# Attention on pairs of key tiles in two adjacent PSUM banks: two double buffers in place of four single ones

## The chip, the cores and the metric

The kernel runs on one core of a Trainium2 chip. The metric is the device time of one execution in microseconds. In a profile, PE is TensorE's matmuls and PEld its weight loads, DVE is VectorE, ACT is ScalarE, POOL is GpSimd, SP is SyncE, which here only issues DMAs. L595 is line 595 of the kernel before.

## The reference

One encoder layer is applied to two requests of 2048 and 256 tokens, which the kernel treats as 2304 tokens in 18 tiles of 128:

```python
p = rmsnorm(x) @ w_in                       # mq mk mv mo gates aq ak av
m_out = mlstm_mixer(mq, mk, mv, mo, gates)  # 8 heads of 64, both directions
a_out = attention_mixer(aq, ak, av)         # 8 query heads, 2 key/value heads of 64
x = x + concat([m_out, a_out]) @ w_out
u = dwconv3(rmsnorm(x) @ w_up);  a, g = split(u)
x = x + (silu(g) * a) @ w_down
```

The attention is a full softmax over the keys of the own request, without a mask:

```python
s = einsum('bqhgd,bkhd->bhgqk', q, k) * HEAD_DIM ** -0.5
o = einsum('bhgqk,bkhd->bqhgd', softmax(s, axis=-1), v)
```

## The kernel before, in words

The program has four phases. Phase A makes queries, keys, values and gates and writes them to DRAM. Then attention runs beside the mLSTM; when the mLSTM has nothing more to issue, phase C (the output projection, its matmuls `po` at L1041) takes its place beside the rest of the attention. Phase D is the feed-forward part.

**Attention.** It is a generator, `attention`, that works through 36 blocks. A block holds four query tiles of 128 (512 query columns) that share a key/value head. 32 blocks are large: their keys are the 16 tiles of the long request. Four are small: two key tiles. Counted from 0, blocks 0, 1, 26 and 27 are small. A large block has eight steps `kp`, each for a pair of key tiles. In a step

- `scores` computes for each key tile z of the pair one score tile `ps` of 128 keys x 512 queries in one PSUM bank, by two matmuls (L595, L596; the second adds the low part and the subtraction of the row maximum). ACT writes the exp in rounded form to `ph` (L599), then the full exp in place (L600), and DVE takes the difference `pl` (L601).
- `maxstep` belongs to the next block: a matmul of queries against 512 keys into `px` (L569) and a maximum over its columns on DVE (L570). A large block needs 16 of them, which are spread over the first steps (the count `k`).
- `values` multiplies `ph` and `pl` of an earlier step by the values, six matmuls into `pv` (L613).

Around a block stand the transposes of the queries into `pq` (L555), the transposed maxima `pr` (L584), and at its end four reciprocals of 64x128 (L630) and a multiplication on POOL. The tiles `ps`, `px`, `pq` and `pr` share one tag of the PSUM pool, with `SCB = 4` buffers of one bank. `ph` and `pl` have six buffers each, that is three steps.

**What sets the order.** `run_both` advances the two generators by the costs that they yield, so that the mLSTM is issued ahead of the attention by a factor `LEAD`. The program is built by a scheduler with a timeline of its own: it takes instructions from the issued order and places one on an engine once its inputs and its buffer are free in that timeline; otherwise a later one goes first. So the order on PE is fixed when the program is built, and PE then runs it strictly in turn. After the mLSTM's last step is issued, PE's order is the one in which the code is written (`manual_schedule`); from there `po` matmuls are dealt out between the attention's steps. The mLSTM's matmuls are `mj`, `mv` (projections, 128x256 each, the bulk), `mS`, `mI`, `mN`, `mu`, `mt`, `mT` (the recurrence).

Of the kernel before, what the change touches and what calls it, by code (L numbers as in the profile page):

```python
# [9 lines left out]
F32 = mybir.dt.float32  # L10
F32R = mybir.dt.float32r
AF = mybir.ActivationFunctionType
ALU = mybir.AluOpType
AX = mybir.AxisListType
# [3 lines left out]
P = 128  # L18
# [11 lines left out]
ACOL = 2048  # L30
MPRI = 2000
STORE = "sync"
SCB = 4
MB = 2
MJ = 1
BLK = 768
# [25 lines left out]
A_MAX = 0.23  # L62
# [9 lines left out]
RW = 4  # L72
PO = 4
PB = 4
PHB = 6
PLB = 6
PLAG = 2
ZT = 3
SG = 3
# [9 lines left out]
def f32(ap):  # L89
    return ap.bitcast(F32)  # L90
# [382 lines left out]
def attention(g, tc, s1, s2, pp):  # L473


    nc = g.nc
    sp = s1
# [13 lines left out]
    def load_kv(grp, k0, k1, after=None):  # L491

        if (grp, k0) in kv:
            return
        n = k1 - k0
        sp = s2 if n == NT1 else s1
        kv[(grp, k0)] = parts = []
        for t0 in range(0, n, 4):
            m = min(4, n - t0)
            s = f"{n}_{t0}"  # L500
            kk = sp.tile([P, m * P], F32R, tag="kk" + s, name=f"kk{grp}_{s}", bufs=1)
            kl1 = sp.tile([65, m * P], F32R, tag="kl1" + s, name=f"kl1{grp}_{s}", bufs=1)
            vs = [sp.tile([P, m, P if a == 0 else HD], F32R, tag=f"v{a}" + s, name=f"v{a}{grp}_{s}", bufs=1)
                  for a in range(2)]
            c = slice((k0 + t0) * P, (k0 + t0 + m) * P)
            if after is not None:
                for t in (kk[0:1, 0:1], kk[HD:HD + 1, 0:1], kl1[0:1, 0:1], vs[0][0:1, 0, 0:1], vs[1][0:1, 0, 0:1]):
                    nc.gpsimd.tensor_copy(t, after[0:1, 0:1])
            nc.gpsimd.memset(f32(vs[0][:, :, HD:]), 1.0)
            for r in (0, HD):  # L510
                nc.gpsimd.dma_start(f32(kk[r:r + HD, :]), g.k_d[grp, 0:HD, c])
            nc.gpsimd.dma_start(f32(kl1[0:HD, :]), g.k_d[grp, HD:P, c])
            nc.gpsimd.memset(f32(kl1[64:65, :]), 1.0)
            for a in range(2):
                nc.gpsimd.dma_start(f32(vs[a][:, :, 0:HD]), g.v_d[a, grp, :, k0 + t0:k0 + t0 + m])
            parts.append((kk, kl1, vs))
# [14 lines left out]
    def load_q(n):  # L531

        if n in qzs or n >= len(hbs):
            return
        t = 0
        qz = qzs[n] = sp.tile([P, 4, P], F32R, tag="qz", name=f"bq{n}", bufs=QZB)
        for h, q0, q1 in hbs[n][1]:
            nc.sync.dma_start(f32(qz[:, t:t + q1 - q0]), g.q_d[q0:q1, :, h].rearrange("n p d -> p n d"))
            t += q1 - q0

    def prep(n):

        s = HB()
        grp, s.qs, k0, k1 = hbs[n]
        load_q(n)
        load_q(n + 1)
        load_kv(grp, k0, k1)
        s.kv = kv[(grp, k0)]
        s.nq, s.nk = 4, k1 - k0
        s.N = s.nq * P  # L550
        s.nm = "%d_%d" % s.qs[0][0:2]
        qz = qzs.pop(n)
        pq = pp.tile([P, 512], F32R, tag="sc", name="pq" + s.nm)
        for t in range(s.nq):
            nc.tensor.transpose(pq[:, t * P:(t + 1) * P], qz[:, t, :], g.identr)  # L555
        s.qq = sp.tile([P, 512], F32R, tag="qq", name="qq" + s.nm, bufs=2)
        nc.scalar.activation(s.qq[:, 0:s.N], f32(pq[:, 0:s.N]), AF.Copy)
        s.qm = sp.tile([65, 512], F32R, tag="qm", name="qm" + s.nm, bufs=2)
        nc.scalar.activation(s.qm[0:HD, 0:s.N], f32(pq[0:HD, 0:s.N]), AF.Copy)
        s.mx = sp.tile([P, 4, 4], F32, tag="mx", name="mx" + s.nm, bufs=2)  # L560
        s.nsp = -(-s.nk * P // 512)
        s.todo = [(t, z) for z in range(s.nsp) for t in range(s.nq)]
        return s

    def maxstep(s):
        t, z0 = s.todo.pop(0)
        w = min(512, s.nk * P - z0 * 512)
        ps = pp.tile([P, 512], F32, tag="sc", name=f"px{s.nm}_{t}_{z0}")
        nc.tensor.matmul(ps[:, 0:w], s.qq[:, t * P:(t + 1) * P], s.kv[z0][0][:, 0:w], start=True, stop=True)  # L569
        nc.vector.tensor_reduce(s.mx[:, t, z0:z0 + 1], ps[:, 0:w], AX.X, ALU.max)  # L570

    def prep2a(s):

        nq = s.nq
        s.m4 = sp.tile([P, 4], F32, tag="m4", name="m4" + s.nm, bufs=2)
        nc.vector.tensor_reduce(s.m4[:, 0:nq], s.mx[:, 0:nq, 0:s.nsp], AX.X, ALU.max)
        s.m4r = sp.tile([P, 4], F32R, tag="m4r", name="m4r" + s.nm, bufs=2)
        nc.vector.tensor_scalar(s.m4r[:, 0:nq], s.m4[:, 0:nq], -1.0, None, ALU.mult)

    def prep2b(s):  # L580

        pr = pp.tile([P, 512], F32, tag="sc", name="pr" + s.nm)
        for t in range(s.nq):
            nc.tensor.matmul(pr[:, t * P:(t + 1) * P], s.m4r[:, t:t + 1].to_broadcast([P, P]), g.identr, start=True,  # L584
                             stop=True)
        nc.scalar.activation(s.qm[HD:HD + 1, 0:s.N], pr[HD:HD + 1, 0:s.N], AF.Copy)

    def scores(s, kp):
        N = s.N
        parts = []  # L590
        for z in range(2):
            ps = pp.tile([P, 512], F32, tag="sc", name=f"ps{s.nm}_{kp}_{z}")[:, 0:N]
            kk, kl1, _ = s.kv[kp // 2]
            kc = (2 * kp + z) % 4 * P
            nc.tensor.matmul(ps, kk[:, kc:kc + P], s.qq[:, 0:N], start=True, stop=False)  # L595
            nc.tensor.matmul(ps, kl1[:, kc:kc + P], s.qm[:, 0:N], start=False, stop=True)  # L596
            ph, pl = (sp.tile([P, 512], F32R, tag=t, name=f"{t}{s.nm}_{kp}_{z}", bufs=n)[:, 0:N]
                      for t, n in (("ph", PHB), ("pl", PLB)))
            nc.scalar.activation(ph, ps, AF.Exp)  # L599
            nc.scalar.activation(ps, ps, AF.Exp)  # L600
            nc.vector.tensor_tensor(pl, ps, f32(ph), ALU.subtract)  # L601
            parts.append((ph, pl))
        return parts

    def values(s, kp, parts):

# [41 lines left out]

    g.a_total = sum(A_PAIR * pairs(b) + A_MAX * 4 * -(-pairs(b) // 2) + A_PREP for b in hbs)
    cur = prep(0)  # L650
    while cur.todo:
        maxstep(cur)
        yield A_MAX
    prep2a(cur)
    prep2b(cur)
    load_kv(0, 0, NT1, cur.m4)
    todo, fins = [], []

    def value():

        s, kp, parts = todo.pop(0)
        values(s, kp, parts)
        if kp == s.nk // 2 - 1:
            while fins:
                fins.pop(0)()
            fin1(s)
            fins.extend([lambda: fin2(s)] * 4 + [lambda: fin3(s), lambda: fin4(s)])

    for n in range(len(hbs)):
        nxt = prep(n + 1) if n + 1 < len(hbs) else None  # L670
        yield A_PREP / 2
        nkp = cur.nk // 2
        ready = None
        for kp in range(nkp):
            todo.append((cur, kp, scores(cur, kp)))
            yield 0.4 * A_PAIR
            if ready:
                prep2b(ready)
                ready = None
            if nxt is not None and nxt.todo:  # L680
                if n == len(hbs) // 2 - 1:

                    k = 2 * (kp - 2) - (nxt.nq * nxt.nsp - len(nxt.todo))
                else:
                    k = -(-len(nxt.todo) // max(nkp - kp - (MXZ if g.alone else MXE), 1))
                for i in range(k):
                    maxstep(nxt)
                    if i % 2:
                        yield 2 * A_MAX
                if not nxt.todo:  # L690
                    prep2a(nxt)
                    ready = nxt
            if len(todo) > PLAG:
                value()
                yield 0.6 * A_PAIR
            for _ in range(1 if kp < nkp - 1 else 2):
                if fins:
                    fins.pop(0)()
        if nxt is not None and nxt.todo:
            while nxt.todo:  # L700
                maxstep(nxt)
# [690 lines left out]
def body(tc, aps, phases="abcd"):  # L1392
# [5 lines left out]
    with ExitStack() as st:  # L1398
# [3 lines left out]
        def pool(stack, name, **kw):  # L1402
            return stack.enter_context(tc.tile_pool(name=name, reuse_waits="tile", **kw))
# [25 lines left out]
        with ExitStack() as s2:  # L1429
# [34 lines left out]
            sa = pool(s2, "b_s", bufs=2)  # L1464
            pa = pool(s2, "b_p", bufs=SCB, space=PSUM)

# [117 lines left out]
```

## Time and profile before

| | |
|---|---|
| three runs, us | 3429.24, 3425.78, 3429.64; median 3429.24 |
| span of the profiled execution, us | 3427.2 (its own time is not listed; the runs' median is 2.0 above the span) |
| busy share PE, DVE, ACT, POOL | 97%, 78%, 56%, 33% |
| instructions | 55596 |
| score matmuls, two per key tile (L595, L596) | 1040 |
| exps (L599, L600), 128x512 | 1040 |
| differences (L601), 128x512 | 520 |
| row maxima (L570) | 528 |

Time runs along the span: phase A until about 250 us, attention beside the mLSTM until about 1400, attention beside phase C until about 1770, then the rest. The row "granted clock" tells at what share of its full speed PE's clock was let through. In the groups, "busy" is the sum over a group, then the mean of one; "idle before" is the time in which the engine stood still just ahead of these instructions, with what ended it.

### The profile page before, as it was taken

What the parts mean: (1) busy time and instruction counts of PE and PEld (TensorE: products, weight loads), DVE (VectorE), ACT (ScalarE), POOL (GpSimd) and SP (SyncE); (2) the same over time, 40 slices, a digit from 0 to 9 for tenths busy, and PEclk for the clock granted to TensorE, in tenths of its full rate; (3) what the DMA queues carried; (4) which work ended last, traced back from release to release, by engine and by line L of the source; (5) the groups of instructions that cost most, each with busy time, mean ns of one, the idle gap of its engine ahead of it and who ended that gap; (6) DMA issues with size and microseconds to landing.
All of it is one profiled execution on the core that took longest, in us unless ns stands there. A gap on an engine that the chain in (4) does not pass through costs nothing. (4 is left out here: it accounts for less than half of the span.)

```text
span 3427.2 us, 55596 instructions
## 1 busy us (share of the span) xinstructions
PE 3329.3 (97%) x20058; PEld 3098.4 (90%) x20058; DVE 2677.3 (78%) x4654; ACT 1931.2 (56%) x4329; POOL 1120.9 (33%) x1328
## 2 busy tenths in 40 slices
PE   7989999999999999899999999999999999999998
PEld 6878888888888888688899999999999999999998
DVE  6885687777768788967767878789888888888776
ACT  4536666666666767655544444446444446555554
POOL 6653132213232323211244333226233224322222
PEclk9999999999999999999999999999999999999999
DMA  6765342333345444422365232223323213421221
GB/s 220 243 203 159 89 140 86 115 123 98 108 131 160 143 123 139 145 77 94 101 216 198 81 105 87 68 80 133 129 94 103 72 59 128 140 74 62 69 74 50
DMA packets 254756, 404.27 MB, mean 118 GB/s; under 512 B 32112, under 2 KB 156816, under 8 KB 254480
## 3 DMA queue, kind: packets, MB, share of 16 engines
q1 hardware_dynamic: 226576, 358.23, 32.7%
q0 software_dynamic: 11344, 33.04, 3.6%
q10 hardware_dynamic: 16560, 9.44, 0.9%
q8 instruction: 158, 2.59, 0.3%
q14 instruction: 118, 0.97, 0.1%
HBM read 316.73 MB, written 83.90 MB: 117 GB/s over the span
## 5 line engine op out<-in xcount | busy, mean ns | idle before, releaser
L1322 PE MATMUL pd<-act,wd 128*128 128x384 f32 (+1 forms) x3120 | 593.4, 336 | 23.9 <-DVE acc L1324 12.6
L1322 PEld LDWEIGHTS pd<-act,wd 128*128 128x128 f32 x3120 | 539.6, 188 | 32.6 <-DVE acc L1324 18.1
L601 DVE TENSOR_TENSOR pl<-ps,ph 128x512 fp32r<-128x512 f32 x520 | 352.7, 683 | 181.5 <-ACT ps L600 173.4
L1184 PE MATMUL pa<-nt,wut 128*128 128x386 f32 (+2 forms) x2376 | 454.3, 339 | 0.0
L599 ACT ACTIVATE ph<-ps 128x512 fp32r<-128x512 f32 x520 | 309.4, 595 | 243.5 <-PE ps L596 239.5
L1184 PEld LDWEIGHTS pa<-nt,wut 128*128 128x128 f32 x2376 | 421.6, 190 | 0.3 <-ACT u L1200 0.3
L570 DVE TENSOR_REDUCE mx<-px 128x1 f32<-128x512 f32 (+1 forms) x528 | 345.5, 670 | 74.4 <-PE px L569 72.4
L1278 DVE SCALAR_TENSOR_TENSOR y<-u,cw,y 128x768 f32<-128x768 f32 (+1 forms) x264 | 315.6, 1196 | 36.4 <-ACT y L1271 29.3
L1189 POOL TENSOR_TENSOR tw<-ru 128x512 f32<-128x512 f32 x66 | 94.1, 1425 | 732.5 <-DMA ru<-w_up 558.5
L613 PE MATMUL pv<-ph,v 128*128 128x512 f32 (+1 forms) x1040 | 319.4, 401 | 1.0 <-ACT ph L599 0.8
L600 ACT ACTIVATE ps<-ps 128x512 f32<-128x512 f32 x520 | 310.3, 597 | 0.0
L1200 ACT ACTIVATE u<-pa 128x386 f32<-128x386 f32 (+2 forms) x264 | 128.3, 486 | 320.9 <-PE pa L1184 320.7
L1324 DVE TENSOR_TENSOR acc<-pd,acc 128x384 f32<-128x384 f32 (+1 forms) x544 | 280.3, 535 | 35.5 <-PE pd L1322 34.1
L1041 PEld LDWEIGHTS po<-cmx,wo 128*128 128x128 f32 x1728 | 220.7, 191 | 8.2 <-DVE mmx L931 0.6
L1041 PE MATMUL po<-cmx,wo 128*128 128x256 f32 x1728 | 224.2, 284 | 0.4 <-DVE mmx L931 0.4
L595 PE MATMUL ps<-qq,kk 128*128 128x512 f32 x520 | 215.5, 416 | 4.2 <-DVE mx L570 2.4
L569 PE MATMUL px<-kk,qq 128*128 128x512 f32 (+1 forms) x528 | 202.8, 413 | 6.0 <-DVE mx L570 2.9
L596 PE MATMUL ps<-qm,kl 65*128 65x512 f32 x520 | 206.7, 399 | 0.0
L759 PE MATMUL mj<-mn,wm 128*128 128x256 f32 x1296 | 203.0, 289 | 2.8 <-ACT og L773 1.9
L759 PEld LDWEIGHTS mj<-mn,wm 128*128 128x128 f32 x1296 | 187.1, 193 | 19.8 <-ACT og L773 2.0
L769 PEld LDWEIGHTS mv<-wm,mn 128*128 128x128 f32 x1296 | 182.8, 190 | 18.4 <-ACT qb L765 2.5
L769 PE MATMUL mv<-wm,mn 128*128 128x256 f32 x1296 | 196.5, 285 | 1.0 <-ACT qb L765 0.9
(288 smaller groups left out, 7266.6 us busy)
## 6 DMA issues: line engine op xcount, KB each, us to landing
ru<-w_up SPq DMA_DIRECT2D x132, 512.0 KB, 3.4
mn<-n_d SPq DMA_DIRECT2D x216, 256.0 KB, 3.4
rd<-w_down SPq DMA_DIRECT2D x66, 512.0 KB, 3.6
n_d<-n1T SPq DMA_DIRECT2D x18, 1024.0 KB, 5.6
dm<-nm_d POOLq DMA_DIRECT2D x72, 256.0 KB, 4.1
mjn<-n_d SPq DMA_DIRECT2D x72, 256.0 KB, 3.3
mvn<-n_d SPq DMA_DIRECT2D x72, 256.0 KB, 3.1
q_d<-qz SPq DMA_DIRECT2D x18, 512.0 KB, 3.7
```

The costliest lines, as they stand in the source:

```text
L570: nc.vector.tensor_reduce(s.mx[:, t, z0:z0 + 1], ps[:, 0:w], AX.X, ALU.max)
L599: nc.scalar.activation(ph, ps, AF.Exp)
L600: nc.scalar.activation(ps, ps, AF.Exp)
L601: nc.vector.tensor_tensor(pl, ps, f32(ph), ALU.subtract)
L613: nc.tensor.matmul(s.pv[0:HD if k in (1, 3) else P, 0:N], v, p, start=(kp == 0 and k == 0), stop=(2 * kp + 2 == s.nk and k == 5))
L759: nc.tensor.matmul(pj[:, o], s.w[c][:, a, o * P:(o + 1) * P], nT[c][:, :, h, :], start=(c + o + k == 0), stop=(c == NCC - 1 and k == 2 and ...
L769: nc.tensor.matmul(pv[:, o], nT[c][:, o, a, :], s.w[c][:, h, 256:512], start=(c + o + k == 0), stop=(c == NCC - 1 and k == 2 and o == 1))
L1041: nc.tensor.matmul(po[:, o], wo[z // 2][c][:, a, n], mx[c][:, h, :], start=(c == 0 and k == 0), stop=(c == NCC - 1 and k == 2))
L1184: nc.tensor.matmul(p, w[:, aa, c, :], ops[k][:, c, bb, 0:n], start=c == 0 and i == 0 and not add, stop=c == NCC // 2 - 1 and i == 2, skip_ ...
L1278: nc.vector.scalar_tensor_tensor(y[:, s:e], u[:, s + k:e + k], cw[:, k, jj:jj + 1], y[:, s:e], ALU.mult, ALU.add)
L1322: nc.tensor.matmul(po, wds[j][c // 4][:, aa, c % 4 * P:(c % 4 + 1) * P], acts[j][:, bb, z0:z1], start=(j == 0 and k == 0), stop=(j == len( ...
L1324: nc.vector.tensor_tensor(accs[c][:, z0:z1], po, accs[c][:, z0:z1], ALU.add)
```

## The change

The two score tiles of a step become one tile of 128x2x512 in two adjacent banks. The four matmuls come first, then one exp to `ph`, one in place and one difference, each on 1024 columns. A `maxstep` takes two query tiles at once: two matmuls into the two banks, one maximum with two results. The shared tag has two buffers of two banks in place of four of one; `pq` and `pr` take a whole double buffer each. `ph` and `pl` have three double buffers. The matmuls stay as they are, in number and shape. `k` and the yields are scaled to the halved number of steps, so that as much cost is yielded as before.

```diff
-SCB = 4
+SCB = 2
-PHB = 6
-PLB = 6
+PHB = 3
+PLB = 3
...
-        pq = pp.tile([P, 512], F32R, tag="sc", name="pq" + s.nm)
+        pq = pp.tile([P, 2, 512], F32R, tag="sc", name="pq" + s.nm)[:, 0]
...
-        s.todo = [(t, z) for z in range(s.nsp) for t in range(s.nq)]
+        s.todo = [(t, z) for z in range(s.nsp) for t in range(0, s.nq, 2)]
...
-        ps = pp.tile([P, 512], F32, tag="sc", name=f"px{s.nm}_{t}_{z0}")
-        nc.tensor.matmul(ps[:, 0:w], s.qq[:, t * P:(t + 1) * P], s.kv[z0][0][:, 0:w], start=True, stop=True)
-        nc.vector.tensor_reduce(s.mx[:, t, z0:z0 + 1], ps[:, 0:w], AX.X, ALU.max)
+        ps = pp.tile([P, 2, 512], F32, tag="sc", name=f"px{s.nm}_{t}_{z0}")
+        for i in range(2):
+            nc.tensor.matmul(ps[:, i, 0:w], s.qq[:, (t + i) * P:(t + i + 1) * P], s.kv[z0][0][:, 0:w], start=True, stop=True)
+        nc.vector.tensor_reduce(s.mx[:, t:t + 2, z0], ps[:, :, 0:w], AX.X, ALU.max)
...
-        parts = []
+        ps = pp.tile([P, 2, 512], F32, tag="sc", name=f"ps{s.nm}_{kp}")[:, :, 0:N]
+        kk, kl1, _ = s.kv[kp // 2]
         for z in range(2):
...
+            nc.tensor.matmul(ps[:, z], kk[:, kc:kc + P], s.qq[:, 0:N], start=True, stop=False)
+            nc.tensor.matmul(ps[:, z], kl1[:, kc:kc + P], s.qm[:, 0:N], start=False, stop=True)
+        ph, pl = (sp.tile([P, 2, 512], F32R, tag=t, name=f"{t}{s.nm}_{kp}", bufs=n)[:, :, 0:N]
+                  for t, n in (("ph", PHB), ("pl", PLB)))
+        nc.scalar.activation(ph, ps, AF.Exp)
+        nc.scalar.activation(ps, ps, AF.Exp)
+        nc.vector.tensor_tensor(pl, ps, f32(ph), ALU.subtract)
+        return [(ph[:, z], pl[:, z]) for z in range(2)]
...
-                    k = 2 * (kp - 2) - (nxt.nq * nxt.nsp - len(nxt.todo))
+                    k = kp - 2 - (nxt.nq // 2 * nxt.nsp - len(nxt.todo))
...
                 for i in range(k):
                     maxstep(nxt)
-                    if i % 2:
-                        yield 2 * A_MAX
+                    yield 2 * A_MAX
```

With the buffers the scheduler's order changes over the whole stage. In the rows below a name holds the query tile at which the block begins, the step, before the change the key tile of the pair, and a running number; `x6` are six instructions of one kind. A wait names the engine whose semaphore is waited for.

PE beside the mLSTM, in the middle of the first key/value head (a block of query tile 4, step 3). Before:

```order
L595 MATMUL ps_4_3_1_5345<-qq_4_4510,kk_16_4_2662 128x512 [waits DVE_49]
L596 MATMUL ps_4_3_1_5345<-qm_4_4512,kl_16_4_2663 128x512
L769 MATMUL mv_1_6038<-wm_2_5222,mn_1_2_5969 128x256 x2
L769 MATMUL mv_1_6038<-wm_3_5223,mn_1_3_5970 128x256 x2
L569 MATMUL px_4_0_3_5365<-kk_16_12_2694,qq_4_5063 128x512 [waits DVE_49]
L769 MATMUL mv_1_6038<-wm_3_5223,mn_1_3_5970 128x256 x4
L769 MATMUL mv_1_6038<-wm_4_5224,mn_1_4_5971 128x256
L838 MATMUL mu_0_6521<-va_0_5280,kw_0_6242 128x130 [waits DVE_49,PE_49,Pool_49]
L769 MATMUL mv_1_6038<-wm_4_5224,mn_1_4_5971 128x256
L569 MATMUL px_4_1_3_5368<-kk_16_12_2694,qq_4_5063 128x512 [waits DVE_49]
```

The same block and step in the changed program:

```order
L596 MATMUL ps_4_3_5015<-qq_4_4282,kk_16_4_2658 128x512 [waits DVE_49]
L597 MATMUL ps_4_3_5015<-qm_4_4284,kl_16_4_2659 128x512
L596 MATMUL ps_4_3_5015<-qq_4_4282,kk_16_4_2658 128x512
L597 MATMUL ps_4_3_5015<-qm_4_4284,kl_16_4_2659 128x512
L613 MATMUL pv_4_5007<-pl_4_2_4866,v_16_4_2660 128x512 x2
L768 MATMUL mv_3_6407<-wm_5_4907,mn_3_5_6341 128x256 x6
L768 MATMUL mv_3_6407<-wm_6_4908,mn_3_6_6342 128x256
L900 MATMUL mN_10_6941<-va_5_2493,dm_10_6204 128x65 [waits DMASW4_49,Activation_49]
L882 MATMUL mS_11_6960<-qb_5_2492,mkT_5_2491 128x256 [waits PE_49,Activation_49]
L900 MATMUL mN_10_6941<-va_5_2493,dm_10_6204 128x65 x3
L571 MATMUL px_4_0_3_5037<-kk_16_12_2690,qq_4_4771 128x512 [waits DVE_49]
L571 MATMUL px_4_0_3_5037<-kk_16_12_2690,qq_4_4771 128x512
```

The attention's matmuls stand in groups, the mLSTM's stand in longer runs between them, and at the same step of the attention the mLSTM is two token blocks further on (`mv_3` in place of `mv_1`).

PE in block 22 of the 36 (second key/value head, query tile 4), from the end of step 0. Before:

```order
L613 MATMUL pv_2_14038<-pl_2_7_1_14337,v_16_12_11389 128x512 [waits DVE_49]
L569 MATMUL px_4_0_0_14432<-kk_16_0_11354,qq_4_14411 128x512 [waits Activation_49]
L838 MATMUL mu_8_15856<-va_4_13637,kw_8_15661 128x130 [waits DVE_49,Pool_49]
L569 MATMUL px_4_1_0_14435<-kk_16_0_11354,qq_4_14411 128x512 [waits Activation_49]
L569 MATMUL px_4_2_0_14438<-kk_16_0_11354,qq_4_14411 128x512 [waits DVE_49]
L838 MATMUL mu_9_15863<-va_4_13637,kw_9_15663 128x130 [waits Activation_49,Pool_49]
L569 MATMUL px_4_3_0_14441<-kk_16_0_11354,qq_4_14411 128x512 [waits DVE_49]
```

The same place in the changed program:

```order
L613 MATMUL pv_2_12756<-pl_2_7_13021,v_16_12_10393 128x512 x2
L571 MATMUL px_4_2_0_13114<-kk_16_0_10358,qq_4_13095 128x512 [waits DVE_49]
L571 MATMUL px_4_2_0_13114<-kk_16_0_10358,qq_4_13095 128x512
L613 MATMUL pv_4_13305<-ph_4_0_13105,v_16_0_10360 128x512 [waits PE_49,Activation_49]
L613 MATMUL pv_4_13305<-ph_4_0_13105,v_16_0_10361 64x512
L613 MATMUL pv_4_13305<-ph_4_0_13105,v_16_0_10360 128x512
L613 MATMUL pv_4_13305<-ph_4_0_13105,v_16_0_10361 64x512
L596 MATMUL ps_4_1_13258<-qq_4_12523,kk_16_0_10358 128x512 [waits DVE_49]
L597 MATMUL ps_4_1_13258<-qm_4_12525,kl_16_0_10359 128x512
L596 MATMUL ps_4_1_13258<-qq_4_12523,kk_16_0_10358 128x512
L597 MATMUL ps_4_1_13258<-qm_4_12525,kl_16_0_10359 128x512
L613 MATMUL pv_4_13305<-pl_4_0_13106,v_16_0_10360 128x512 x2
```

No mLSTM matmul is left here: in the changed order the last one (`mT_17` of the last head pair) stands in block 21, before the change in block 28. From block 22 to the first `po`, which in both programs stands in block 28, PE has attention alone.

DVE at the same place, from the first row maximum of step 0. Before:

```order
L570 TENSOR_REDUCE mx_4_14415<-px_4_2_0_14438 128x1 [waits PE_49]
L570 TENSOR_REDUCE mx_4_14415<-px_4_3_0_14441 128x1 [waits PE_49]
L630 RECIPROCAL rs_2_14619<-rs_2_14619 64x128 [waits Activation_49]
L630 RECIPROCAL rs_2_14619<-rs_2_14619 64x128 x3
L849 SCALAR_TENSOR_TENSOR C_9_13614<-C_8_13613,dec,C_9_13614 128x65 [waits Activation_49]
L601 TENSOR_TENSOR pl_4_1_0_14588<-ps_4_1_0_14584,ph_4_1_0_14587 128x512 [waits Activation_49]
```

In the changed program:

```order
L602 TENSOR_TENSOR pl_4_0_13106<-ps_4_0_13100,ph_4_0_13105 128x1024 [waits Activation_49]
L572 TENSOR_REDUCE mx_4_13099<-px_4_2_0_13114 128x2 [waits PE_49]
L630 RECIPROCAL rs_2_13283<-rs_2_13283 64x128 [waits Activation_49]
L630 RECIPROCAL rs_2_13283<-rs_2_13283 64x128 x3
L572 TENSOR_REDUCE mx_4_13099<-px_4_0_1_13268 128x2 [waits PE_49]
L602 TENSOR_TENSOR pl_4_1_13264<-ps_4_1_13258,ph_4_1_13263 128x1024 [waits Activation_49]
```

The four reciprocals stand in one piece in both; in the changed program they and a maximum stand ahead of the difference that frees the score buffer of step 1.

More of the change, by code (lines that the diff above doesn't have):

```diff
@@ L580, in prep2b @@
     def prep2b(s):
-        pr = pp.tile([P, 512], F32, tag="sc", name="pr" + s.nm)
+        pr = pp.tile([P, 2, 512], F32, tag="sc", name="pr" + s.nm)[:, 0]
         for t in range(s.nq):
@@ L589, in scores @@
         N = s.N
-        parts = []
+        ps = pp.tile([P, 2, 512], F32, tag="sc", name=f"ps{s.nm}_{kp}")[:, :, 0:N]
+        kk, kl1, _ = s.kv[kp // 2]
         for z in range(2):
-            ps = pp.tile([P, 512], F32, tag="sc", name=f"ps{s.nm}_{kp}_{z}")[:, 0:N]
-            kk, kl1, _ = s.kv[kp // 2]
             kc = (2 * kp + z) % 4 * P
[L595 to L603, printed above, removed]
+            nc.tensor.matmul(ps[:, z], kk[:, kc:kc + P], s.qq[:, 0:N], start=True, stop=False)
[6 more added lines that the diff above has]
+        return [(ph[:, z], pl[:, z]) for z in range(2)]
     def values(s, kp, parts):
@@ L652, in attention @@
         maxstep(cur)
-        yield A_MAX
+        yield 2 * A_MAX
     prep2a(cur)
@@ L687, in attention @@
                     maxstep(nxt)
-                    if i % 2:
-                        yield 2 * A_MAX
+                    yield 2 * A_MAX
                 if not nxt.todo:
```

## The prediction

> **What bounds the kernel now.** I read the head of the page first, then the busy times by stage, then what PE waits for in each stage.
>
> ```profile
> span 3427.2 us, 55596 instructions
> ...
> PE 3329.3 (97%) x20058; PEld 3098.4 (90%) x20058; DVE 2677.3 (78%) x4654; ACT 1931.2 (56%) x4329; POOL 1120.9 (33%) x1328
> ```
>
> The busy times of three stretches (busy and count for PE, PEld, DVE, ACT, POOL, then granted clock and DMA share):
>
> ```profile
> 400.00:1390.00 990.00, 986.13 (x6255) 863.84 (x6254) 771.41 (x1718) 674.78 (x1821) 284.34 (x577) 1.00 0.42 125
> 1390.00:1460.00 70.00, 59.43 (x292) 45.43 (x290) 63.61 (x151) 44.75 (x112) 10.47 (x20) 0.88 0.44 129
> 1460.00:1770.00 310.00, 305.41 (x1928) 268.22 (x1927) 215.66 (x371) 163.29 (x324) 63.90 (x67) 0.99 0.32 103
> ```
>
> PE stands still for only 3.9 us of the 990 in which attention has mLSTM work beside it. So there the time is PE's work, and DVE (78% busy) and ACT (68%) can become shorter without any gain. The one weak place is 1390 to 1460: the mLSTM runs out, PE is busy for 59.4 of 70 us, at a clock of 0.88, and DVE is the full engine with 63.6. PE's waits there, from the longest:
>
> ```profile
> PE mN L901 <- DVE mmx L931: 3.1, 1, 3.1
> PE px L569 <- DVE mx L570: 2.0, 4, 0.8
> ```
>
> This is what attention costs when nothing fills its waits. The 10.6 us of idle time and about 6 us by the lower clock (0.12 of 70 us is 8.4, part of it idle anyway) make some 16 us that PE loses there.
>
> **The removed cost.** The groups of the instructions that are merged:
>
> ```profile
> L601 DVE TENSOR_TENSOR pl<-ps,ph 128x512 fp32r<-128x512 f32 x520 | 352.7, 683 | 181.5 <-ACT ps L600 173.4
> ...
> L599 ACT ACTIVATE ph<-ps 128x512 fp32r<-128x512 f32 x520 | 309.4, 595 | 243.5 <-PE ps L596 239.5
> ...
> L570 DVE TENSOR_REDUCE mx<-px 128x1 f32<-128x512 f32 (+1 forms) x528 | 345.5, 670 | 74.4 <-PE px L569 72.4
> ```
>
> No operation on 1024 PSUM columns exists here, so I price it from other widths, by shape:
>
> ```profile
> L570 DVE TENSOR_REDUCE mx<-px 128x1 f32<-128x256 f32 x16 | 6.4, 418 | 2.1 <-PE px L569 1.6
> L254 ACT ACTIVATE qk<-pj 128x640 f32<-128x640 f32 x18 | 12.6, 701 | 19.3 <-DVE xh L273 9.9 <-PE pj L245 5.1 <-DMA mn<-n_d 3.1
> L186 ACT ACTIVATE xq<-x 128x1024 f32<-128x1024 f32 x16 | 16.8, 1060 | 28.5 <-DMA x<-xT 28.4
> L200 DVE TENSOR_TENSOR x<-x,rs_a 128x1024 f32<-128x1024 f32 x16 | 19.3, 1210 | 9.9 <-PE rs_a L142 9.9
> L630 DVE RECIPROCAL rs<-rs 64x128 f32<-64x128 f32 x144 | 122.4, 901 | 7.7 <-ACT rs L622 7.4
> L108 ACT ACTIVATE wo<-ro 128x512 fp32r<-128x512 f32 x16 | 9.9, 629 | 9.6 <-DMA ro<-w_out 9.0 <-PE mv L785 0.4
> L110 DVE TENSOR_TENSOR wo<-ro,wo 128x512 fp32r<-128x512 f32 x16 | 10.8, 686 | 1.9 <-ACT wo L108 1.8
> ```
>
> ACT: (701 - 595) over 128 columns is 0.83 ns a column, so 1024 columns take 1.02 us; the 640-column row crosses a bank, the 1024-column row (SBUF) gives 1.06 as upper bound. I take 1.02. DVE: the 512-wide maxima are 678 once the 16 narrow ones are taken out, so 260 ns for 256 columns and 1.2 us for 1024; the SBUF row says 1.21. Saved on paper: 260 x (2 x 683 - 1200) = 43 us and 264 x (2 x 678 - 1200) = 41 us of DVE, 520 x (2 x 595 - 1020) = 88 us of ACT. All of it is beside PE, which is busy in 986 of 990 us. I count it as zero; should that cover fail, the matter is the bare stage below. The mLSTM's loads on SP and POOL come earlier, with the same count; at a DMA share of 0.42 that costs nothing.
>
> **The added cost: a longer chain for a buffer.** How a step runs now, on PE, ACT and DVE:
>
> ```profile
> 1475.29 0.39 PE L595 MATMUL ps<-qq,kk 128*128 128x512 f32 x1
> 1475.52 0.40 PE L596 MATMUL ps<-qm,kl 65*128 65x512 f32 x1
> 1475.76 0.40 PE L595 MATMUL ps<-qq,kk 128*128 128x512 f32 x1
> 1476.00 0.40 PE L596 MATMUL ps<-qm,kl 65*128 65x512 f32 x1
> ```
>
> ```profile
> 1476.02 0.60 ACT L599 ACTIVATE ph<-ps 128x512 fp32r<-128x512 f32 x1 [3.02 <-PE ps L596]
> 1476.51 0.60 ACT L600 ACTIVATE ps<-ps 128x512 f32<-128x512 f32 x1
> 1477.03 0.59 ACT L599 ACTIVATE ph<-ps 128x512 fp32r<-128x512 f32 x1
> ```
>
> ```profile
> 1425.33 0.62 DVE L570 TENSOR_REDUCE mx<-px 128x1 f32<-128x512 f32 x1
> ...
> 1426.00 0.50 PE L595 MATMUL ps<-qq,kk 128*128 128x512 f32 x1 [1.29 <-DVE mx L570]
> ```
>
> Matmuls of 512 columns start every 0.235 us; ACT starts 0.10 after a score tile's end (1475.92) and the second exp 0.1 before the first one's end; PE starts 0.05 after DVE. A score tile of two banks thus needs: last matmul's end 3 x 0.235 + 0.40 = 1.10, then 0.10, exps 0.92 + 1.02, to 3.14; difference 0.04 + 1.20, to 4.38; next use at 4.43 us after its start. A `px` tile needs 0.24 + 0.40 + 0.04 + 1.2 + 0.05 = 1.9 us. Before, a single-bank score tile needed 0.64 + 0.1 + 0.5 + 0.6 + 0.04 + 0.68 + 0.05 = 2.6, with four buffers.
>
> *The stage with mLSTM work.* In the quoted rows of query tile 4 the score buffer is used again 39 matmuls after the tile's last one. At this stage's mean of 990/6255 = 0.158 us that is 6.2 us of work against 4.43 - 0.94 = 3.5 needed. So no wait is added where the runs are like this one: 0 us, with a bound of 60 us (below).
>
> *The bare stage.* The price of that order is that the mLSTM is used up by block 21. A large block of attention alone is 96 matmuls x 0.235 plus about 1 us for `pq` and `pr`, 23.5 us of PE work. Steps 0 to 3: score tiles come one chain apart, 4.43 us, for 14 matmuls (3.3 us); two `px` and the difference on DVE, 3.6 us, fit in. In step 1 four reciprocals (3.6 us) stand ahead of the difference; about 1 us of it falls in DVE's free time: +2.6. Together 20.3. Steps 4 to 7: two buffers, 2.2 us a step by the chain, 2.35 by PE (10 matmuls); I take 2.4, together 9.6. Change of block about 1. Sum 31.0, so 7.5 lost in each block:
>
> - blocks 22, 23, 24: 3 x 7.5 = 22;
> - block 21: 7.5, and eight weight splits of phase C on ACT (8 x 0.63) and DVE (8 x 0.69) put between its exps: +5, so 12;
> - blocks 25 to 28 until `po` begins: block 25 has no `px` of 512 columns but the reciprocals, 5; the small block 26 waits for its maxima and `pr`, 3; block 27 makes eight double `px` for block 28, 8 x 1.2 on DVE against 3.8 on PE, 7; five steps of block 28, 5: together 20;
> - the lower clock about block 27 (6, as now) and about 1 us in each bare block: 10.
>
> That is 64 us. The 16 us now lost at this place are replaced by it: +48. The least that the bare stage can cost is where chains overlap until DVE (16 x 1.2 + 3.6 = 22.8) or PE (23.5) is full: 1 us a block, some 25 in all with the small blocks and the clock, +9 net. The most is half clock throughout, below.
>
> *Blocks 17 to 20.* Some of the score buffers there are used again after only 2 to 3 us of matmuls: 59 score tiles, a quarter short by about 1.1 us, part of which coincides: +10 (0 to 20).
>
> *Beside phase C.* In 1460 to 1770 PE lost 4.6 us. Step 0 of a block has two `px` in a row on one buffer, a wait of some 1.2 us in each of seven blocks, 8: +4. In the other steps a buffer is used again after more than 4 us, no cost.
>
> Sum: 48 + 10 + 4 = +62. The profiled span is 3427.2, 2.0 below the median of the three runs (3425.78 to 3429.64); on the median the forecast is **3491 us**.
>
> [...] How the clock went in the bare part of today's kernel, in 10 us stretches:
>
> ```profile
> 1400.00:1410.00 10.00, 6.69 (x28) 5.79 (x27) 9.54 (x29) 4.55 (x12) 2.62 (x5) 0.50 0.40 108
> 1410.00:1420.00 10.00, 8.84 (x45) 6.23 (x44) 9.25 (x26) 7.45 (x25) 2.62 (x6) 1.00 0.08 24
> 1420.00:1430.00 10.00, 7.80 (x29) 5.13 (x28) 9.95 (x24) 5.81 (x14) 3.36 (x5) 0.86 0.09 25
> ```
>
> At 67% busy the clock was half, at 78% 0.86, at 88% full. The bare blocks would be 23.5/31 = 76% busy, 74% in steps 0 to 3. [...] The rows above agree that idling brings half clock in pieces; none shows it for a whole block. [...]
>
> **The rivals.**
>
> 1. *Forecast: the bare stage appears, the rest stays covered.* 3491. Chance 0.62.
> 2. *The filled stage waits too.* DVE, 78% busy there and in strict order, makes the difference late by the length of a maximum or a reciprocal. If each of some 175 steps lost 0.35 us: +60, 3551. Against it: 6.2 us of room for 3.5 of need, and only 3.9 us lost now. It decides from about 2.7 us of delay in a step. 0.12.
> 3. *Half clock in the bare blocks.* PE's work doubles to 47 us a block; with 31 already counted that is +16 in four blocks: 3491 + 64 = 3555. For it the row at 0.50, against it the row at 0.86. 0.08.
> 4. *The bare stage is nearly hidden.* Chains overlap as in the lower bound: +9 to +11, 3439. 0.10; as little again that it is within measurement, 0.03.
> 5. *Faster.* Between 1390 and 1460 DVE is the full engine and releases PE. If the merged operations (166 ns less for each difference, 156 for each maximum) let DVE keep up there and the bare blocks run at PE's pace, the 16 us lost now come back: 3413. It decides if a bare block takes under 24 us. Against it: a chain of 4.43 us for 3.3 us of PE work. 0.05.
>
> **The numbers.** I take +-0.2% (7 us) as what a measurement can tell from no change: slower 0.92, within 0.03, faster 0.05. The likeliest case alone spans 3465 to 3520. The range of 8 in 10 reaches down to the hidden bare stage (3445) and up into cases 2 and 3 (3550).
>
> **What would show it.** The profile after should have PE over 97% busy until about 1260 us (the mLSTM ends seven blocks earlier), then some 150 us with PE at 70 to 80%, waits of `ps` for the difference and of `px` for the maximum as its longest, and a full DVE nowhere. Exps of 1.02 us and DVE operations of 1.2 us would confirm the prices; a large block of 31 us the chain. Score tiles in bare steps less than 4 us apart would refute it, waits of PE for `pl` before 1000 us would mean case 2, a mean clock under 0.7 in the bare stage case 3. The forecast is wrong most easily in the pace of the bare block, on which three quarters of it rest.

## The result and the profile after

The changed kernel takes 3524.51 us (median of four runs, 3523.27 to 3525.50) against 3428.76 for the kernel before: a ratio of 1.0282 (95% interval 1.0268 to 1.0297), 96 us slower. The forecast was 3491 within 3445 to 3550. Side and range held, the size was a third too small.

The head of the page after, whose rows answer to the first ones of before:

```profile
span 3521.6 us, 54551 instructions
...
PE 3368.3 (96%) x20058; PEld 3098.3 (88%) x20058; DVE 2642.9 (75%) x4130; ACT 1894.7 (54%) x3809; POOL 1108.5 (31%) x1328
```

DVE has 524 and ACT 520 instructions fewer, and is busy for 34 and 37 us less. The prediction's paper savings (84 and 88) were too large, since it added up durations: in its own rows the second exp starts 0.1 us before the first one's end, and that overlap goes with the merging. PE has the same 20058 matmuls, and is "busy" for 39 us more: a matmul that starts after a wait, or at the lower clock, is drawn longer (of 128x512 in this run: 0.50 us after a wait of over 0.2 us and 0.63 at half clock, 0.40 otherwise, each the median). So the busy share hides a part of the loss, and the events tell it better. The last mLSTM matmul (`mT`) and the `po` matmuls of phase C, of before and then of after (minimum, median and maximum duration, then first and last start):

```profile
L926 PE MATMUL mT<-ident,hh x72: 270/272/447, 466.6 to 1439.4; 128*128 128x128 f32 x72
L1041 PE MATMUL po<-cmx,wo x1728: 274/283/419, 1440.1 to 1830.3; 128*128 128x256 f32 x192
```

```profile
L925 PE MATMUL mT<-ident,hh x72: 270/272/415, 448.0 to 1319.3; 128*128 128x128 f32 x72
L1040 PE MATMUL po<-cmx,wo x1728: 274/283/419, 1519.9 to 1929.5; 128*128 128x256 f32 x192
```

The mLSTM ends 120 us earlier and `po` begins 80 us later; between them lie 200 us of bare attention, that is attention with no other matmuls beside it. The `po` stage itself takes 410 in place of 390 us. Behind it little changed: 1597 and 1592 us from the last `po` to the end. The same three stages by busy time, of before and of after (columns as in the prediction):

```profile
250.00:1390.00 1140.00, 1133.59 (x7237) 994.98 (x7237) 861.52 (x1884) 764.49 (x2051) 331.14 (x679) 1.00 0.43 127
1390.00:1440.00 50.00, 40.59 (x187) 29.90 (x185) 47.55 (x121) 29.68 (x81) 10.47 (x20) 0.86 0.24 71
1440.00:1835.00 395.00, 388.59 (x2556) 347.88 (x2557) 267.15 (x457) 198.70 (x391) 95.09 (x92) 0.99 0.42 134
```

```profile
250.00:1320.00 1070.00, 1051.87 (x6851) 926.93 (x6850) 751.95 (x1454) 658.76 (x1602) 324.68 (x678) 1.00 0.45 136
1320.00:1520.00 200.00, 160.40 (x581) 100.95 (x580) 135.96 (x149) 111.50 (x140) 16.65 (x21) 0.91 0.14 41
1520.00:1934.00 414.00, 392.77 (x2560) 349.55 (x2559) 251.87 (x334) 184.85 (x260) 94.07 (x91) 0.99 0.35 115
```

To count the whole loss, I took from the trace the distance from each matmul's start to the next one's, and subtracted the usual distance for its number of columns (the lower quartile of the profile before: 0.230 us for 512 columns, 0.118 for 256). Both kernels run the same matmuls, so the usual distances add up to the same 3148 us. What is over is time lost, here in the stages of the rows above:

| us lost | mLSTM stage | between (weak / bare) | `po` stage | sum |
|---|---|---|---|---|
| before | 98 | 22 | 20 | 141 |
| after | 123 | 77 | 39 | 239 |
| difference | +24 | +55 | +19 | +98 |
| forecast | +10 | +48 | +4 | +62 |

Some 98 us of loss beside the mLSTM are there with either kernel; only the difference is the change's. Before and behind these stages the changed kernel loses 4 us less, which gives the 94 us between the two spans. The longest waits of PE in the bare stage (us in total, times, the longest):

```profile
PE px L571 <- DVE mx L572: 10.1, 13, 2.2
PE ps L596 <- DVE pl L602: 8.9, 15, 1.0
PE pv L613 <- ACT rs L622: 4.7, 5, 1.7
PE pv L613 <- ACT ph L600: 4.3, 11, 1.2
PE ps L596 <- DVE mx L572: 4.3, 3, 2.8
PE ps L596 <- ACT qm L588: 2.7, 7, 0.9
```

And in the `po` stage after it, from 1520 to 1934:

```profile
PE ps L596 <- DVE mx L572: 5.9, 4, 3.2
PE px L571 <- DVE mx L572: 5.3, 4, 1.3
```

### The profile page after: what moved, and what is told of

Its sections match the earlier page's. It is cut to its first block, busy times and chain, and to the rows that moved or that the text cites. A ratio compares the mean times of both kernels' runs of the same rounds, so it can differ in the third digit from the quotient of the medians.

```text
span 3521.6 us, 54551 instructions
## 1 busy us (share of the span) xinstructions
PE 3368.3 (96%) x20058; PEld 3098.3 (88%) x20058; DVE 2642.9 (75%) x4130; ACT 1894.7 (54%) x3809; POOL 1108.5 (31%) x1328
## 3 DMA queue, kind: packets, MB, share of 16 engines
q1 hardware_dynamic: 226576, 358.23, 31.6%
## 5 line engine op out<-in xcount | busy, mean ns | idle before, releaser
L572 DVE TENSOR_REDUCE mx<-px 128x2 f32<-128x1024 f32 (+1 forms) x264 | 316.4, 1201 | 173.3 <-PE px L571 172.5
L600 ACT ACTIVATE ph<-ps 128x1024 fp32r<-128x1024 f32 x260 | 266.2, 1024 | 334.7 <-PE ps L597 333.5
L602 DVE TENSOR_TENSOR pl<-ps,ph 128x1024 fp32r<-128x1024 f32 x260 | 316.7, 1218 | 160.6 <-ACT ps L601 158.2
L613 PE MATMUL pv<-ph,v 128*128 128x512 f32 (+1 forms) x1040 | 295.2, 405 | 12.5 <-ACT rs L622 6.8
L601 ACT ACTIVATE ps<-ps 128x1024 f32<-128x1024 f32 x260 | 265.1, 1020 | 0.0
L613 PEld LDWEIGHTS pv<-ph,v 128*128 128x128 f32 (+1 forms) x1040 | 157.4, 164 | 71.2 <-ACT ph L600 14.9
L571 PE MATMUL px<-kk,qq 128*128 128x512 f32 (+1 forms) x528 | 180.3, 424 | 23.2 <-DVE mx L572 19.3
L758 PE MATMUL mj<-mn,wm 128*128 128x256 f32 x1296 | 185.2, 289 | 3.2 <-ACT og L772 2.2
L768 PE MATMUL mv<-wm,mn 128*128 128x256 f32 x1296 | 184.9, 287 | 0.6 <-ACT qb L764 0.4
L758 PEld LDWEIGHTS mj<-mn,wm 128*128 128x128 f32 x1296 | 172.5, 193 | 13.4 <-ACT og L772 2.9
```

The lines of the kernel that those rows point to most:

```text
L572: nc.vector.tensor_reduce(s.mx[:, t:t + 2, z0], ps[:, :, 0:w], AX.X, ALU.max)
L613: nc.tensor.matmul(s.pv[0:HD if k in (1, 3) else P, 0:N], v, p, start=(kp == 0 and k == 0), stop=(2 * kp + 2 == s.nk and k == 5))
L758: nc.tensor.matmul(pj[:, o], s.w[c][:, a, o * P:(o + 1) * P], nT[c][:, :, h, :], start=(c + o + k == 0), stop=(c == NCC - 1 and k == 2 and ...
```

## The experiments

Theory A was the prediction's: the loss is the bare stage, which arises because the mLSTM is placed ahead and used up. Its rival B (theory C in the expectations of e5 to e8 is its sharper form) was that two buffers in turn cost at each step, so that attention waits wherever little lies beside it. "Before" below is the kernel before on the same chip.

**e1: no bare stage.**

```diff
-LEAD = 1.3
+LEAD = 1.7
...
+    yield 0, 0.0
     nxt = loads(0, 0)
```

> The changed kernel with LEAD 1.7 in place of 1.3 (the first po then stands in PE's order about half a block behind the last mLSTM matmul, in block 21, in place of seven blocks later; phase C's first loads wait until its rows are finished). Theory A (the loss is the bare stage between the mLSTM's end and the first po, where attention alone waits for its two buffers): the bare stage goes, phase C's work is spread over 14 blocks, each of which may lose 2 to 3 us: 3455 us, 3440 to 3475. Theory B (the longer chain of the double buffers costs at every step, and filler used at one place is missing at another): 3500 to 3530, as the changed kernel. If merging is free once the filler lies right, 3430 or less.

Measured: 3512.31 us, before 3424.38, ratio 1.0256 (1.0240 to 1.0271). The first `po` starts at 1344.4, 30 us behind the last `mT`, and yet nearly all of the loss is there. Theory A's 3455 failed. From 1315 to 1927:

```profile
1315.00:1927.00 612.00, 557.95 (x3196) 460.73 (x3194) 399.45 (x496) 303.51 (x411) 116.08 (x116) 0.97 0.29 92
```

```profile
PE ps L596 <- DVE mx L572: 21.7, 15, 3.5
PE px L571 <- DVE mx L572: 17.2, 14, 2.1
```

By the measure above 102 us are lost in these 612, where after loses 116 in the bare and the `po` stage together. So the loss does not need blocks with nothing at all beside them: the same `po` work, spread over 14 blocks in place of eight, leaves it nearly as large. Whether the buffers or the thin spreading make it, this run does not tell; e4, e10 and e11 below bear on that.

**e2: three single buffers, nothing merged.**

```diff
-SCB = 4
+SCB = 3
```

> The kernel before with three single-bank buffers in place of four, nothing merged. Theory A (the number of buffers in turn decides how far the mLSTM is placed ahead, and so where its work runs out; the width of the operations does not matter): the last mLSTM matmul stands in block 20 here, blocks 21 to 27 are bare and lose about 5 us each, DVE being full in their first steps: 3470 us, 3450 to 3500. Rival (the wide operations are what costs): no change, 3425 to 3435.

3548.65 us, before 3424.38, ratio 1.0354 (1.0333 to 1.0374): outside the range on the slow side. The direction is as theory A and B have it, the wide operations are not needed for a loss. The last `mT` starts at 1304.5, the first `po` at 1525.9, the last at 1955.6: a bare stage of 221 us, and a `po` stage of 430 us, where I had counted nothing. The number of buffers alone thus moves the mLSTM's end. The large bare blocks 22 to 24 take 30.4 to 30.6 us, some 7 over PE's 23.5, where I had put 5.

**e3 and e4: all blocks from 22 on bare, in the order of the code.** For both kernels (LEAD 1.8 and 2.2, so that the last `mT` stands in block 21 in both):

```diff
-C_LEAD = 12.0
+C_LEAD = 1e9
...
             have = min(have + (s or 0) * pace, 2 * cost)
+        for _ in c:
+            pass
```

with e1's line ahead of the loads.

> The changed kernel with the mLSTM issued early (LEAD 1.8) and all of phase C behind the attention, so that blocks 22 to 35 are bare, with PE in the order of the code. Theory A: a large bare block takes 31 to 33 us against 23.5 of PE work, the total 3585 us (3560 to 3620). Waits of ps for the difference and of px for the maximum lead the list. If the half clock belonged to bare blocks as such, they would be over 45 us and the total over 3700.

> The same for the kernel before (LEAD 2.2, phase C behind the attention): blocks 22 to 35 bare with four single-bank buffers. Theory A (two double buffers make the bare block long): PE's 23.5 us or DVE's 25.4 (32 operations of 0.68 and four reciprocals of 0.9) bound a large block: 26 us (25 to 28), total 3450 (3440 to 3480). Rival (any attention without filler takes over 30 us, whatever the buffers): 31 to 33 us a block, total above 3530.

e3: 3571.66 us, e4: 3524.04, one run each (before 3424.38). e3 came out 13 us under the expected 3585 (within its range), e4 44 us over the upper end of its own. Large bare blocks from 22 on take 31.6 to 34.3 us with the double buffers, about as expected, but 29.0 to 30.4 with four single ones, where I expected 26 and the rival 31 to 33 (without block 25, which has no maxima of 512 columns, and block 28, which follows the small ones). So of the 8 to 11 us over PE's 23.5, the double buffers cost some 3; about 6 come with either kind of buffer. Over the whole bare stage (1312 to 1748 and 1317 to 1702) 144 us are lost in e3 and 99 in e4. Where a part of the 6 comes from, in the timeline of one block of e4 (start, duration), on DVE and then on PE:

```profile
1539.97 3.37 DVE L630 RECIPROCAL rs<-rs 64x128 f32<-64x128 f32 x4
1543.26 0.62 DVE L570 TENSOR_REDUCE mx<-px 128x1 f32<-128x512 f32 x1
```

```profile
1541.17 0.40 PE L596 MATMUL ps<-qm,kl 65*128 65x512 f32 x1
1543.94 0.50 PE L595 MATMUL ps<-qq,kk 128*128 128x512 f32 x1 [2.36 <-DVE mx L570]
...
1547.54 0.63 PE L595 MATMUL ps<-qq,kk 128*128 128x512 f32 x1
1547.97 0.63 PE L596 MATMUL ps<-qm,kl 65*128 65x512 f32 x1
...
1551.20 0.40 PE L595 MATMUL ps<-qq,kk 128*128 128x512 f32 x1
1551.43 0.39 PE L596 MATMUL ps<-qm,kl 65*128 65x512 f32 x1
```

A maximum stands behind four reciprocals on DVE and PE waits 2.36 us for its buffer. About 2 us later the matmuls start 0.43 us apart in place of 0.23, from 1546.26 to 1549.25; with the two at the edges that is some 1.6 us more. The granted clock is 0.66 there (columns as in the prediction):

```profile
1545.00:1550.00 5.00, 4.91 (x15) 3.69 (x15) 2.69 (x6) 2.15 (x5) 1.11 (x2) 0.66 0.12 26
```

I had left out both the queue and the clock.

**e5 and e6: PE in the order of the code from the start**, so that the mLSTM lasts until block 28 in both.

```diff
     with ExitStack() as st:
+        st.enter_context(tc.manual_schedule(engines={mybir.EngineType.PE}))
         while dm is not None:
...
         g.alone = True
-        st.enter_context(tc.manual_schedule(engines={mybir.EngineType.PE}))
```

> The changed kernel with PE held to the order in which the code is written from the beginning of the attention on (so far only after the mLSTM's last step); the last mLSTM matmul then stands in block 28, right ahead of the first po, as in the kernel before. Theory A (the loss comes from the mLSTM running ahead and leaving bare blocks): within 15 us of e6, the same order with four single buffers. Theory C (a block of attention is bound by the turn of its two buffers wherever it stands, and the running ahead is only what the order makes of that): 60 us or more above e6. The absolute time depends on what the mLSTM's own waits cost in this order, which no run shows so far; I take 3460 to 3600.

> The kernel before with PE in the order of the code from the beginning of the attention on: the measure for e5. The mLSTM's recurrence waits where other work was put in between before; 3440 to 3560.

4004.47 and 3873.94 us, before 3424.25: ratios 1.1695 (1.1678 to 1.1713) and 1.1311 (1.1294 to 1.1328). Both are far above what I expected: in this order the recurrence waits in the open (`mu` for ACT's `C`: 58 us in each). The difference, 131 us, speaks for B: without any running ahead, `px` waits 152.4 us for the maxima with the double buffers (up to the last `mT`) and 82.5 with the single ones. But with so much else waiting it is no price for the kernel as it is.

**e7: the double buffers with single-bank operations.**

```diff
-        nc.scalar.activation(ph, ps, AF.Exp)
-        nc.scalar.activation(ps, ps, AF.Exp)
-        nc.vector.tensor_tensor(pl, ps, f32(ph), ALU.subtract)
+        for z in range(2):
+            nc.scalar.activation(ph[:, z], ps[:, z], AF.Exp)
+            nc.scalar.activation(ps[:, z], ps[:, z], AF.Exp)
+            nc.vector.tensor_tensor(pl[:, z], ps[:, z], f32(ph[:, z]), ALU.subtract)
```

and the maxima likewise.

> The changed kernel's buffers (two of two banks) with the operations of before: exps, differences and maxima of one bank each, so nothing is merged. A score tile is free again after 0.64 + 0.1 + 4 x 0.5 + 0.1 + 0.04 + 0.68 = 3.6 us in place of 4.4, since the second bank's exps run beside the first one's difference. Theory A and C (buffers, not width): no better than the changed kernel, though a bare block may take 29 in place of 33 us; the last mLSTM matmul stands in block 18 here, so there are three more bare blocks: 3500 to 3540. Rival (the wide operations are what costs): 3430 to 3450.

3594.14 us, before 3424.25, ratio 1.0495 (1.0478 to 1.0513), slower than any theory gave. The cost is thus there without the wide operations; with two double buffers the merged form is the better one. A bare block takes 37 to 38 us, not 29, since my chain was wrong. ACT in one step:

```profile
1366.88 0.60 ACT L602 ACTIVATE ph<-ps 128x512 fp32r<-128x512 f32 x1 [0.47 <-PE ps L598]
1367.37 0.59 ACT L603 ACTIVATE ps<-ps 128x512 f32<-128x512 f32 x1
1368.72 0.60 ACT L602 ACTIVATE ph<-ps 128x512 fp32r<-128x512 f32 x1 [0.76 <-DVE pl L604]
1369.21 0.59 ACT L603 ACTIVATE ps<-ps 128x512 f32<-128x512 f32 x1
```

The second bank's exp waits 0.76 us for the first bank's difference: the program orders them by the tile, not by its halves. The tile is held for 5.0 us (1365.62 to 1370.62 on PE). So e7 prices this form, not unmerged operations as such.

**e12: only the maxima unmerged** (two reductions of 512 columns on the double tile).

> The changed kernel with two maxima of one bank in place of the one of two banks; exps and differences stay merged, the order on PE is the same. A px tile is held 0.16 us longer. e7 (nothing merged) was 70 us slower than the changed kernel; if the merged exps and differences carry that, this is 3540 us (3525 to 3555); if the maxima carry it, 3570 or more.

3531.29 us, before 3424.24, ratio 1.0306 (1.0290 to 1.0322) against 1.0282 for the changed kernel: within the first range. The intervals overlap, so the 8 us between the two are hardly clear of noise. By elimination, most of e7's distance then belongs to the exps and differences, and to the serial order just shown.

**e8 and e9: without reciprocals**, in the changed kernel and in the kernel before.

```diff
-            nc.vector.reciprocal(r, r)
+            pass
```

> The changed kernel without the four reciprocals of each block (left out; the rows are multiplied by the sums themselves): DVE has 3.6 us a block less, and nothing long stands ahead of a difference or a maximum. If the reciprocals are what makes the double buffers late (each bare block loses some 3 us by them), a bare block takes 30 us and the total 3485 (3470 to 3505). If the turn of the two buffers alone decides: 3510 or more.

> The kernel before without its reciprocals (left out as in e8): the measure for e8's gain of 37 us. With four single buffers DVE's work is beside PE nearly everywhere; only the 16 us lost at the mLSTM's end can shrink: 3415 us (3408 to 3425). Rival (the reciprocals cost the same in both kernels, and have nothing to do with the double buffers): 3395 or less.

e8: 3487.54 us (one run), before 3424.25: a ratio of 1.0185 against 1.0282, some 33 us less, the number that the queue theory gave. Its bare stage loses 58 us in place of 77 and its `po` stage 25 in place of 39; the mLSTM stage loses as much as in the changed kernel (122 and 123). The number is in part luck: a bare block takes 31.7 us (expected 30) in place of 33.0, so the reciprocals cost it 1.3 us and not 3. The order moved as well: the last `mT` starts at 1339.4 in place of 1319.3 and the first `po` at 1500.9 in place of 1519.9, so that about one bare block fewer is left. PE's waits from the mLSTM's end to the last `po` no longer have `ps` behind a maximum among the first:

```profile
PE px L571 <- DVE mx L572: 10.5, 12, 1.3
PE ps L596 <- DVE pl L602: 6.3, 11, 1.0
```

e9: 3427.64 us, before 3424.24, ratio 1.0008 (0.9999 to 1.0017): no change, and not the 3415 I expected. It is no clean control, because the built order moves here too, in the other direction: attention gets ahead, block 28 begins at about 1354, and until 1447 the mLSTM's tail has only 12 score tiles beside it, where the mLSTM stage usually has some 30 in such a time; PE is busy for 76 of 87 us:

```profile
1360.00:1447.00 87.00, 75.86 (x480) 67.64 (x478) 65.15 (x190) 47.14 (x151) 27.77 (x55) 0.86 0.53 164
```

Ahead of this stretch and behind it nothing was gained either: 97 us are lost from 250 to 1360 and 21 in the `po` stage, where the kernel before loses 98 (to 1390) and 20. So the gain of the `po` stage in e8 goes with the double buffers.

**e10 and e11: a better place for the change of work in the kernel before?** LEAD 1.35 and 1.4.

> The kernel before with LEAD 1.35: the mLSTM's last step and the first po move from block 28 to block 27, so that the two small blocks have po beside them or close behind. If the weak place is worth what it seems (some 16 us), a part of it returns: 3418 us (3410 to 3430). If it is the mLSTM's own tail that waits, no change: 3425.

> The same with LEAD 1.4: the change from mLSTM to po stands in block 25, before the small blocks, which then have po beside them: 3420 us (3408 to 3440); over 3440 if the thinner po leaves attention's waits open as in e1.

3440.42 us (ratio 1.0048, 1.0036 to 1.0061) and 3455.76 (1.0090, 1.0076 to 1.0104), before 3424.24: both slower, by 0.5 and 0.9%. The mLSTM ends earlier (last `mT` at 1423.4 and 1407.9 in place of 1439.4), but the last `po` later (1846.2 and 1866.5 in place of 1830.3). The `po` stages of e10 and of e11:

```profile
1423.50:1851.00 427.50, 412.34 (x2644) 363.31 (x2645) 288.42 (x491) 215.05 (x423) 99.08 (x98) 0.99 0.39 125
1408.00:1871.00 463.00, 440.67 (x2740) 383.13 (x2740) 310.63 (x533) 232.02 (x454) 105.05 (x101) 0.97 0.37 118
```

PE stands idle for 15 and 22 us of them, against 6 of the 395 before. By the measure above they lose 34 and 51 us in place of 20, while up to the last `mT` 122 us are lost in both and 120 before. So with four single buffers too, `po` spread over more attention leaves more waits open. I found no version that beats the kernel before.

## Why the prediction was right or wrong

**Right: side and place.** The work of DVE and ACT that was saved made no stage shorter. The new order left the mLSTM's end in block 21 and a bare stage behind it, the largest term: forecast +48, measured +55. PE waits longest for `px` and `ps`, as forecast, and DVE is not full there (136 of 200 us). The stage came later and is longer than I wrote: from 1319 for 200 us, not from 1260 for some 150. The lower clock also takes more: 0.91 over 200 us is up to 18 us (part of them idle anyway), where I had put 10.

**Right: the prices.** The merged operations on 1024 PSUM columns, which the trace of before did not show:

```profile
L600 ACT ACTIVATE ph<-ps 128x1024 fp32r<-128x1024 f32 x260 | 266.2, 1024 | 334.7 <-PE ps L597 333.5
L601 ACT ACTIVATE ps<-ps 128x1024 f32<-128x1024 f32 x260 | 265.1, 1020 | 0.0
L602 DVE TENSOR_TENSOR pl<-ps,ph 128x1024 fp32r<-128x1024 f32 x260 | 316.7, 1218 | 160.6 <-ACT ps L601 158.2
```

1.02 and 1.2 us had been put down from the widths beside them.

**Nearly right: the bare block.** One score tile of block 23 and the next use of its buffer, on PE, ACT and DVE:

```profile
1388.89 0.50 PE L596 MATMUL ps<-qq,kk 128*128 128x512 f32 x1 [0.40 <-DVE pl L602]
1389.23 0.39 PE L597 MATMUL ps<-qm,kl 65*128 65x512 f32 x1
...
1393.46 0.50 PE L596 MATMUL ps<-qq,kk 128*128 128x512 f32 x1 [0.40 <-DVE pl L602]
...
1397.38 0.50 PE L596 MATMUL ps<-qq,kk 128*128 128x512 f32 x1 [0.33 <-ACT qm L588]
```

```profile
1390.18 1.03 ACT L600 ACTIVATE ph<-ps 128x1024 fp32r<-128x1024 f32 x1 [2.69 <-PE ps L597]
1391.11 1.02 ACT L601 ACTIVATE ps<-ps 128x1024 f32<-128x1024 f32 x1
...
1395.69 1.02 ACT L601 ACTIVATE ps<-ps 128x1024 f32<-128x1024 f32 x1
1396.73 0.59 ACT L588 ACTIVATE qm<-pr 1x512 fp32r<-1x512 f32 x1
```

```profile
1392.19 1.21 DVE L602 TENSOR_TENSOR pl<-ps,ph 128x1024 fp32r<-128x1024 f32 x1
```

From 1388.89 to 1393.46 are 4.57 us; the forecast was 4.43. The 0.1 more is the start: the first matmul after a wait takes 0.50, and the second starts 0.34 after it, not 0.235. Steps 0 to 3 of this block took 20.3 us (1373.15 to 1393.46), the forecast's number, but by luck: the four steps took 5.4, 5.7, 4.6 and 4.6 us, and I had 4.4, 7.0, 4.4 and 4.4. The reciprocals in step 1 cost about half of the 2.6 us that I had put down, and the two `px` of step 0, which I had let fit in, cost about 1 us. Steps 4 to 7 with the change of block took 12.7 (1360.47 to 1373.15 in block 22) and not 10.6: I let two score tiles overlap there, but step 5 waits until 1397.38, because the other buffer is held by `pr`, whose copy `qm` stands on ACT behind both exps of step 4. A whole block thus takes 33.0 us (`pq` at 1371.4, 1404.4 and 1437.7) and not 31.0. I had put this hold into "change of block about 1".

**Wrong: the terms outside the bare stage.** +14 us were forecast there, and +43 of the 98 were measured.

- *The mLSTM stage,* +24 in place of +10. I took 0 for blocks up to 16, by one place where 6.2 us of work stood against a need of 3.5, and kept a bound of 60 for it. Block for block, blocks 2 to 16 lose 80 us in place of 52 and blocks 17 to 20 29 in place of 16, though each of them now also holds more mLSTM work, and the stage has seven blocks fewer. So the 10 for blocks 17 to 20 was about right, and the 0 was wrong. PE's idle time in the stage grew from 6 to 18 us by the rows above, with `px` for the maximum as the longest wait (4.0 us). Rival 2 had the place, at under half its price, but its sign did not show: before 1000 us PE waited for `pl` once, for 0.3 us.
- *The `po` stage,* +19 in place of +4. I had counted two `px` in a row (PE waited 5.3 us for that) and not DVE's order: a maximum or difference behind four reciprocals holds a buffer, and with only two of them PE stands (`ps` for a maximum, 5.9 us, the longest wait 3.2). e8, without the reciprocals, lost 14 us less in this stage.

**The theory behind it held in half.** I took the missing work beside attention for the whole cause. e1 put `po` right behind the mLSTM and got back only some 9 of 96 us (ratio 1.0256 against 1.0282), so that filling the bare blocks thinly is no cure. But that does not clear the order, since e10 and e11 lose by thinner `po` with four single buffers too. What the buffers do in a bare block, and what bareness does, shows in blocks 22 to 27 (from the `pq` written at the start of block 22 to the one at the start of block 28), in which PE has attention alone in all four of these runs:

| run | buffers | us |
|---|---|---|
| after | two double | 154.6 |
| e3, order of the code | two double | 145.5 |
| e2 | three single | 141.6 |
| e4, order of the code | four single | 132.0 |

So of the 77 us lost in the bare stage, some 14 to 23 hang on the double buffers; this is an estimate from the differences to e4, since the order is not the same in these runs. The larger part would be lost with four single buffers as well, once the mLSTM is used up that early. That it is used up early does come from the buffers: in e2 only their number was changed, and the last `mT` moved to 1304.5. With the same two double buffers, a longer hold makes the block dearer: 33.0 us at a hold of 4.57 us, 37 to 38 at 5.0 (e7). How the loss beside the mLSTM and beside `po` divides between buffers and order is not settled: in e5 and e6, where the order was held, other waits cover it, and no run issued the changed kernel's mLSTM later (a lower LEAD).

**Half clock in the bare blocks (rival 3) did not come.** Blocks 22 to 25, with PE at 79 to 85%, had the full clock or nearly (0.96 in 1400 to 1440); only around block 27 it fell, as before the change:

```profile
1400.00:1410.00 10.00, 8.06 (x34) 5.10 (x33) 5.46 (x5) 7.91 (x11) 0.00 (x0) 1.00 0.09 27
1470.00:1480.00 10.00, 6.19 (x21) 3.53 (x21) 7.94 (x11) 4.67 (x7) 3.58 (x4) 0.67 0.13 39
1480.00:1490.00 10.00, 8.06 (x14) 3.30 (x14) 9.23 (x9) 0.00 (x0) 1.15 (x3) 0.50 0.06 13
```

Waits of 0.2 to 1.2 us at each step of blocks 22 to 25 went with half clock once only, for 3.4 us (granted clock 0.66 in 1410 to 1415); behind longer single waits it came more often (below).

## What to carry to other kernels

Merging operations over two PSUM banks halves the number of tiles in flight (here from four to two): before saving instructions on engines that are hidden anyway, price the hold of a buffer (last matmul to last reader) against the number of buffers, with every tile that shares the tag and every piece in the queue of the engine that frees it. Where two streams share an engine by a built order, look at where each runs out, before and after; and where you move other work to the place that waits, make the same move in the kernel before, or its own cost is taken for the change's.

## What the runs showed of the hardware that I had not expected

Behind long single waits of PE the lower clock followed. Between 1320 and 1934 in after, three waits of over 2.2 us began at the full granted clock: 2.81 us ahead of the matmul at 1508.86, 3.20 ahead of the one at 1744.37 and 3.78 ahead of the one at 1855.62. Each had half clock by 3 us behind its end (granted clock 0.83 in 1505 to 1515, 0.83 in 1740 to 1750, 0.75 in 1850 to 1860). Of eight waits between 1.3 and 2.2 us there, one had; of 46 between 0.3 and 1.3 us, five. The kernel before has two like them in phase D, of 2.46 us (ahead of 2337.24) and 2.31 us (ahead of 2860.52), with a granted clock of 0.83 in 2335 to 2345 and in 2855 to 2865. It did not follow each such wait: in after the granted clock was 1.00 in 415 to 425, around a wait of 2.24 us (ahead of 418.73), and in 2957 to 2967, around one of 2.44 us (ahead of 2961.80). This is a count of what followed, not a test in which the wait alone was changed. In the block of e4 shown above, behind its wait of 2.36 us, the granted clock was 0.66 from 1545 to 1550, which is 3.4 us at half, so that the wait cost some 1.6 us more.
